# Low halves of woven weights by an adding DMA, with a changed planner, in a two-layer encoder trunk

## The chip, the cores and the metric

The kernel runs on one core of a Trainium2 chip. The metric is the device time of one execution in microseconds. The kernel before takes 1692.75 us (median of three runs, 1692.19 to 1692.83). Besides these times there is one profiled execution, from which all rows below are taken.

Engine names as in the profile: PE is TensorE (matrix products; PEld its weight loads), DVE is VectorE, ACT is ScalarE, POOL is GpSimd, SP is SyncE, which issues the DMAs.

## The reference

Two requests of 512 tokens by 1024 features go through two layers with the same weights. Cut to what matters:

```python
# layer 0: RWKV-7 time mixing, in both directions
r, k, v = lerp(0) @ w_r, lerp(1) @ w_k, lerp(2) @ w_v
z = xn @ w_z
for d in range(2):                 # forward and backward, each its own decay and rate
    ys.append(_wkv7_scan(r, decay, k_d, v, -kk, kk * a, reverse=(d == 1)))
out = (group_norm(ys[0] + ys[1]) + bonus) * silu(z)
x = x + rms_norm(out @ w_o)
# layer 1: 2-D neighbourhood attention over an 8 x 64 grid
q, k, v, z = split(xn @ w_in + b_in, 4)
o = attention in a window of 8 x 16 tokens with a relative bias
x = x + rms_norm((o * silu(z)) @ w_ao + b_o)
```

All values are 32-bit floats. Every dense product here has 1024 x 1024 weights per output block of 1024 columns.

## The kernel before

A dense product is made of three products in a reduced 32-bit format: each operand x is split in a high half, x rounded to that format, and a low half, x minus the high half. High by high, high by low and low by high are summed in PSUM. A column of a dense product is 128 output features of 512 tokens. It takes 8 steps over the features, with 3 products of 128x128 by 128x512 each. Its weights come as two loads of 128x512 (256 KB) into tiles `raw` (three buffers). Each load is split into a pair `whi`, `wlo` (four buffers of each, `NW`), which serves four steps.

There are 144 columns for the two requests' projections, and the last output projections beside them. They run in three stages:

- A prelude (to about 172 us): norms, token shifts, the small low-rank products, and two sets of columns for the first request.
- The woven stage (172 to 1172 us). The scan of layer 0 runs in 8 groups (two requests, four blocks of heads) of 8 steps each. `prep` makes the scan's operands for a head pair, `inverse` inverts triangular blocks by elimination (lines 941 and 942, 30 dependent pairs of VectorE instructions per group), and `step` runs one scan step (products L1106, L1112, L1133, L1153 and L1157, with ScalarE's copies Z and X between them and VectorE's state S). `finish` normalises a group. Beside all this `flow` makes 76 columns of dense products: r and v of the first request, k, r, v and z of the second, the first request's output projection of layer 0, and the first `NPA` of eight sets of four columns of its layer-1 input projection. `NPA` is 5.
- The rest (1172 to 1694 us): the remaining columns, and attention, whose steps are given out between products at fixed rates (`POST0` 0.7 steps per step of an input column, `POST` 1.0 per step of an output column; what is left comes behind them).

The order of PE, DVE and ACT in the woven stage is written out by a planner. Each piece of work is a Python generator, a `Thread` with a rank. A `yield` names the engine of what comes next, and may give a gate (a condition that must hold) and a time at which operands are ready. `weave` keeps a `Clock` with modelled costs and ends of every instruction. It gives the next turn to a thread whose work can start about now, engines other than PE first, then by rank. Products of `flow` have the rank 9 and so fill what the scan leaves free. `Clock.LAT` is what the model adds between an engine's end and a reader on another engine; `one` holds the costs per instruction (`n` is the number of elements per partition). The queues of SP and POOL are not written out: the building library sets their order.

`splits` in `flow` is the part that the change is about. A half may be split once its load is issued and the pair four halves back has been used (`did["k"] // 4 + NW`). ScalarE copies `raw` into the high half (L703). VectorE subtracts it from `raw` into the low half (L705). Only then may `products` set the steps that read it (L751 to L753). `splits` has rank 3 when no more than one half is in stock, else 9. POOL has only small memsets in this stage: the padding column of `prep`'s exponentials (L841) and parts of `MT` (L959).

In the rest the same split is made by `halves` (L355, L356), and the products by `gemm` (L406 to L408); neither is changed.

Of the kernel before, what the change touches and what calls it, by code (L numbers as in the profile page):

```python
# [11 lines left out]
F32 = mybir.dt.float32  # L12
F32R = mybir.dt.float32r
AF = mybir.ActivationFunctionType
ALU = mybir.AluOpType
# [4 lines left out]
P = 128  # L20
T = 512
D = 1024
# [28 lines left out]
class Clock:  # L51
# [1 line left out]


    ENG = {"PE": "P", "Activation": "A", "DVE": "D", "Pool": "G", "SP": "S"}
    LAT = dict(P=200.0, A=45.0, D=45.0, G=90.0, S=0.0)
    BANKS = ("pf", "zy", "us", "pm", "pg", "pt", "po")

    def __init__(self, nc):
# [52 lines left out]
    def one(self, e, i):  # L112
        ap = lambda xs: [x for x in xs if hasattr(x, "bass_ap")]
        outs, ins = ap(i.outs), ap(i.ins)
        if not outs:
            return 0.0
        name = lambda x: x.bass_ap.tensor.name
        t = issued = self.t[e]
        for table, xs in ((self.made, ins), (self.used, outs)):
            for x in xs:  # L120
                for f, at in table.get(name(x), {}).items():
                    if f != e or e == "S":
                        t = max(t, at)
        free = lambda x: int(np.prod([n for _, n in x.ap[1:]])) if len(x.ap) > 1 else 1
        n = max([free(outs[0])] + [free(x) for x in ins[:1]])
        if e == "P":
            t, done = self.matmul(i, ins, free(outs[0]), t)
        elif e == "S":

            self.t[e] = issued = max(issued, self.t["P"]) + 380.0  # L130
            size = outs[0].ap[0][1] * free(outs[0]) * 4
            c = size * 0.0027 + 150.0
            self.dq = max(issued + 800.0, self.dq) + c
            done = max(self.dq, t + 800.0 + c) + 670.0
        else:
            if e == "A":
                c = 175.0 + 0.86 * n
            elif e == "G":
                c = 150.0 + n
            else:  # L140
                kind = type(i).__name__
                sb = [x for x in ins if free(x) > 8 and not name(x).startswith(self.BANKS)]
                c = 80.0 + 1.06 * n
                if "Reciprocal" in kind:
                    c = 80.0 + 6.2 * n
                elif getattr(i, "is_tensor_tensor_scan", False):
                    c = 80.0 + 2.1 * n
                elif "Transpose" in kind:
                    c = 80.0 + 1.8 * n
                elif len(sb) == 1 and len(ins) <= 2 and "TensorTensor" not in kind and "Reduce" not in kind and free(outs[0]) == n:  # L150
                    c = 110.0 + 0.53 * n if not getattr(i, "is_scalar_tensor_tensor", False) else 130.0 + 1.06 * n
            self.t[e] = t + c
            done = t + c + self.LAT[e]
        for x in ins:
            u = self.used.setdefault(name(x), {})
            u[e] = max(u.get(e, 0.0), done)
            self.slot[name(x)] = True
        for x in outs:
            for table in (self.used, self.made):
                u = table.setdefault(name(x), {})  # L160
                u[e] = max(u.get(e, 0.0), done)
        return 0.0 if e == "S" and "dram" in str(type(outs[0].bass_ap.tensor)).lower() else done
# [51 lines left out]

class Trunk:
    NACT, NW, NRAW, NXR, NTMP, WP = 18, 4, 3, 3, 5, 512
    POST0, POST, POST2, POST3, NPA = 0.7, 1.0, 0.15, 0.66, 5
    HP, HS = (1000, 0), 1000
    OUT1 = ("pg", "pg", "pg", "pg")
    HPA = 1000  # L220
# [460 lines left out]
    def flow(self):  # L681


        nc, did, ck = self.nc, self.did, self.clock
        cols = [(g, j, src, done) for g, (_, _, c) in enumerate(self.groups) for j, (src, done) in enumerate(c)]
        name = lambda *xs: [x.tensor.name for x in xs]
        raw, w, x, todo = {}, {}, {}, {}
# [11 lines left out]
        def splits():  # L699
            for h in range(2 * len(cols)):  # L700
                yield "A", lambda: h < did["load"] and h < did["k"] // 4 + self.NW, lambda c: c.at(name(raw[h]))
                hi, lo = (self.t(tag, (P, self.WP), self.NW, F32R) for tag in ("whi", "wlo"))
                nc.scalar.copy(hi, raw[h])  # L703
                yield "D"
                nc.vector.tensor_tensor(lo, raw.pop(h), hi.bitcast(F32), op=ALU.subtract)  # L705
                w[h] = hi, lo
                did["split"] += 1

# [50 lines left out]
        def posts(a):  # L759
# [4 lines left out]

        few = lambda: did["split"] - did["k"] // 4 <= self.STOCK
        return [
            Thread(lambda: 0, loads()), Thread(lambda: 3 if few() else 9, splits()), Thread(lambda: 0, fetched()), Thread(lambda: 2.5, operands()),
            Thread(lambda: 9, products()), Thread(lambda: 2, posts(0)), Thread(lambda: 2, posts(1))]


    def prep(self, s, p):
# [139 lines left out]
        ks = kps[0]  # L911
        yield "D"
        vt.tensor_tensor(ks, kps[0], kps[1], op=ALU.add)
        vt.scalar_tensor_tensor(ks, ks, self.vec("rk", p), r, op0=ALU.mult, op1=ALU.mult)
        self.save("ks", s, p, ks)

# [5 lines left out]
    def inverse(self, s, pb):  # L922

        nc = self.nc
        vt, gps, act = nc.vector, nc.gpsimd, nc.scalar
        f = lambda tag, shape: self.t(tag, shape, 1, F32, self.front)
        wc, Gd, Go = self.formed[s, pb]
        NU = 32
        free, room = self.bank()
        need = lambda *xs: lambda c, n=[x.tensor.name for x in xs]: c.at(n)  # L930
        gd, go = (x.rearrange("p h i g t -> p (h i g) t") for x in (Gd, Go))
        yield "D", None, need(Gd)
        N = f("N", (P, 32, 32))
        vt.transpose(N, gd.rearrange("p u t -> p t u"))
        tmp = f("etmp", (P, 256))
        self.did["gd"] += 1
        for q in range(1, 31):
            n = 31 - q
            tv = tmp[:, :n * q].rearrange("p (i j) -> p i j", i=n)
            yield "D"  # L940
            vt.tensor_tensor(tv, N[:, q + 1:, q:q + 1].broadcast_to([P, n, q]), N[:, q:q + 1, :q].broadcast_to([P, n, q]), op=ALU.mult)  # L941
            vt.tensor_tensor(N[:, q + 1:, :q], tv, N[:, q + 1:, :q], op=ALU.add)  # L942
        yield "D"
        vt.tensor_tensor(N, N, self.lower, op=ALU.mult)
        vt.memset(N.rearrange("p i j -> p (i j)")[:, 0:1024:33], 1.0)

        yield "D"
        NA = f("NA", (P, NU, 32))
        vt.transpose(NA.rearrange("p u j -> p j u"), N.rearrange("p i j -> p j i"))
        MT = self.MTb[self.nM % 2]  # L950
        self.nM += 1

        yield "D"
        vt.transpose(MT[:, :, 0, :].rearrange("p u i -> p i u"), N)
        yield "A"
        for q in (1, 3):
            r = slice(32 * q, 32 * q + 32)
            act.copy(MT[r, :, 1], MT[r, :, 0])
            gps.memset(MT[r, :, 0], 0.0)  # L959
        for step in range(2):  # L960
            for j0 in (0, 16):
                us = slice(j0, j0 + 16)
                yield "P", free, (lambda c: max(room(c), need(NA)(c))) if step == 0 else (lambda c: max(room(c), need(MT)(c)))
                ps = self.p("pm", (P, 16, 32))
                for j in range(16):
                    for h in range(2):
                        x, y = slice(64 * h, 64 * h + 32), slice(64 * h + 32, 64 * h + 64)
                        u = j0 + j
                        if step == 0:
                            nc.tensor.matmul(ps[y, j], go[x, u], NA[x, u], start=True, stop=True, tile_position=(64 * h, 64 * h + 32))  # L970
                        else:
                            nc.tensor.matmul(ps[x, j], NA[y, u], MT[y, u, 1], start=True, stop=True, tile_position=(64 * h + 32, 64 * h))
                yield "A", None, need(ps)
                for h in range(2):
                    if step == 0:
                        y = slice(64 * h + 32, 64 * h + 64)
                        act.copy(NA[y, us], ps[y])
                    else:
                        x = slice(64 * h, 64 * h + 32)
                        act.copy(MT[x, us, 1], ps[x])  # L980
        self.formed[s, pb] = wc, MT
# [98 lines left out]
    def step(self, q):  # L1080
# [16 lines left out]
        ab, e = st.ab, st.e  # L1097
# [60 lines left out]
        if not st.last:  # L1158
# [3 lines left out]
            if st.i == 0:  # L1162
                vt.tensor_tensor(st.S, so, wc, op=ALU.mult)
            else:
                vt.tensor_tensor(st.S, so, before.S, op=ALU.add)
                vt.tensor_tensor(st.S, st.S, wc, op=ALU.mult)

        yi = st.y[:, min(st.i, 7 - st.i)]
# [11 lines left out]
    def finish(self, s, pb, y):  # L1180
# [14 lines left out]
        bc = lambda t: t.unsqueeze(2).broadcast_to([P, 16, HD])  # L1195
        yield "D", None, need(y)
        vt.tensor_reduce(st[:, 0], yv, axis=AX.X, op=ALU.add)
        vt.tensor_scalar(st[:, 1], st[:, 0], -1.0 / HD, None, op0=ALU.mult)
        yield "D"
        vt.tensor_tensor(yv, yv, bc(st[:, 1]), op=ALU.add)  # L1200
# [654 lines left out]
```

## Time and profile before

| what | value |
|---|---|
| median of the runs shown | 1692.75 us |
| profiled execution | 1695.69 us, span 1693.9 us |
| mean granted TensorE clock | 0.958 |
| PE, DVE, ACT, POOL busy in the span | 91%, 73%, 58%, 1% |
| PE busy in the woven stage, 172 to 1172 us | 879.44 us of 1000 |
| moved by DMA | 336.23 MB, 198 GB/s on the mean |

In a row of a group stand its line, engine, operation and tiles, its shape and count, then busy us and mean ns of one, and the idle time of its engine just before, with what ended it. In a row of waits stand who waited, for whom, us in total, times, and the longest. A row of a stretch gives busy us of each engine with the number of instructions, then the granted clock, the share of the DMA engines and GB/s. A row of DMA issues ends with the median us from issue to landing. Busy times of one group are those of a profiled execution whose PE ends are modelled.

### The profile page before, as it was taken

How to read it: one execution, taken by the hardware profiler on the slowest of the kernel's cores; microseconds unless marked ns; L12 is line 12 of the kernel's file. 1: busy time of each engine (PE TensorE's matmuls, PEld its weight loads, DVE VectorE, ACT ScalarE, POOL GpSimd, SP SyncE). 2: the span in 40 equal slices, each digit the busy share in tenths (PEclk: the TensorE clock that was granted, in tenths of full speed). 3: DMA queues.
4: the chain of work that ended last, by engine and by line, in shares of the span. 5: the costliest groups of instructions: out<-in, count | busy, mean ns of one | idle time of the engine just before them, and what ended most of it. 6: DMA issues, size and time to landing. Idle time of an engine off the chain costs nothing.

```text
span 1693.9 us, 45876 instructions
## 1 busy us (share of the span) xinstructions
PE 1542.3 (91%) x18624; PEld 1171.7 (69%) x18624; DVE 1243.6 (73%) x2725; ACT 987.9 (58%) x1979; POOL 24.1 (1%) x94
## 2 busy tenths in 40 slices
PE   7989788889998988889978689999999999999998
PEld 6767556666676766666656477777777887777776
DVE  8985679688786886897878988656566686555564
ACT  5443655767665666667576545544567765555562
POOL 0000000000000000000000000000000000000000
PEclk9989989899999999999989799999999999999999
DMA  5435687786686777885667754557555346545553
GB/s 207 162 124 187 201 286 222 209 257 224 196 258 197 233 230 220 273 262 188 210 226 233 225 181 141 158 169 261 177 184 181 113 138 240 188 155 174 168 175 106
DMA packets 240819, 336.23 MB, mean 198 GB/s; under 512 B 53696, under 2 KB 119360, under 8 KB 240608
## 3 DMA queue, kind: packets, MB, share of 16 engines
q1 hardware_dynamic: 240608, 333.31, 61.2%
q8 instruction: 146, 2.39, 0.6%
q14 instruction: 65, 0.53, 0.1%
HBM read 227.71 MB, written 105.51 MB: 197 GB/s over the span
## 4 chain that ended last, share of the span: by engine, by line
PE 59%; DVE 16%; DMA 9%; ACT 9%; issue 5%; SPq 1%; DVEq 0%; ACTq 0%
PE pg L406 6%; PE pg L407 6%; PE pg L408 6%; PE pm L751 5%; PE pm L752 4%; PE pm L753 4%; PE sc L1375 2%; PE pf L1035 2%; PE po L1408 2%; DVE etmp L941 2%; DVE N L942 2%; PE pt L1393 1%; PE zy L1106 1%; DVE wlo L705 1%; PE us L1133 1%
## 5 line engine op out<-in xcount | busy, mean ns | idle before, releaser
L751 PE MATMUL pm<-act,whi 128*128 128x512 f32 x608 | 272.5, 448 | 19.4 <-ACT whi L703 8.9
L753 PE MATMUL pm<-act,wlo 128*128 128x512 f32 x608 | 249.2, 410 | 13.3 <-DVE wlo L705 11.9
L752 PE MATMUL pm<-act,whi 128*128 128x512 f32 x608 | 248.6, 409 | 11.2 <-DVE act L731 8.3
L406 PE MATMUL pg<-act,whi 128*128 128x512 f32 x480 | 199.8, 417 | 0.0
L407 PE MATMUL pg<-act,whi 128*128 128x512 f32 x480 | 190.2, 396 | 0.0
L408 PE MATMUL pg<-act,wlo 128*128 128x512 f32 x480 | 189.8, 396 | 0.0
L355 ACT CAST whi<-raw 128x512 fp32r<-128x512 f32 x156 | 96.4, 619 | 134.8 <-PE pg L407 87.9
L751 PEld LDWEIGHTS pm<-act,whi 128*128 128x128 f32 x608 | 119.2, 196 | 60.5 <-issue 13.3
L753 PEld LDWEIGHTS pm<-act,wlo 128*128 128x128 f32 x608 | 119.3, 196 | 50.0 <-DVE wlo L705 19.4
L356 DVE TENSOR_TENSOR wlo<-raw,whi 128x512 fp32r<-128x512 f32 x156 | 106.7, 686 | 59.8 <-ACT whi L355 49.8
L752 PEld LDWEIGHTS pm<-act,whi 128*128 128x128 f32 x608 | 119.7, 197 | 34.8 <-DVE act L731 11.4
L705 DVE TENSOR_TENSOR wlo<-raw,whi 128x512 fp32r<-128x512 f32 x152 | 103.3, 684 | 46.8 <-ACT whi L703 43.7
L703 ACT CAST whi<-raw 128x512 fp32r<-128x512 f32 x152 | 93.1, 618 | 31.4 <-PE pm L752 13.1
L408 PEld LDWEIGHTS pg<-act,wlo 128*128 128x128 f32 x480 | 90.7, 189 | 19.9 <-issue 0.7
L406 PEld LDWEIGHTS pg<-act,whi 128*128 128x128 f32 x480 | 90.9, 189 | 19.4 <-issue 4.8
L407 PEld LDWEIGHTS pg<-act,whi 128*128 128x128 f32 x480 | 91.0, 190 | 17.2 <-issue 3.0
L942 DVE TENSOR_TENSOR N<-etmp,N 128x30 f32<-128x30 f32 (+14 forms) x240 | 79.7, 332 | 8.2
L941 DVE TENSOR_TENSOR etmp<-N 128x30 f32<-128x30 f32 (+14 forms) x240 | 78.4, 327 | 4.5
L1386 DVE CUSTOM_DVE_ANT_0 sb<-sc,bias 128x256 f32<-128x256 f32 x128 | 50.5, 420 | 39.8 <-PE pt L1393 29.2
L1389 ACT ACTIVATE sb<-sb,mx 128x256 f32<-128x256 f32 x128 | 64.2, 503 | 16.4 <-DVE mx L1388 16.0
L1035 PE MATMUL pf<-cab 64*64 64x128 f32 (+1 forms) x2048 | 69.9, 274 | 3.7 <-issue 3.1
L1145 ACT COPY X<-us 64x256 f32<-64x256 f32 x128 | 46.8, 366 | 33.7 <-PE zy L1013 31.2
(381 smaller groups left out, 3298.3 us busy)
## 6 DMA issues: line engine op xcount, KB each, us to landing
dab<-ab SPq DMA_DIRECT2D x32, 1024.0 KB, 7.3
cab<-dab SPq DMA_DIRECT2D x64, 512.0 KB, 4.3
raw<-in_w_in_dram SPq DMA_DIRECT2D x128, 256.0 KB, 3.4
bias<-in_rpb_dram SPq DMA_DIRECT2D x32, 384.0 KB, 4.1
raw<-in_w_z_dram SPq DMA_DIRECT2D x32, 256.0 KB, 5.3
dz<-tmp SPq DMA_DIRECT2D x32, 256.0 KB, 3.3
raw<-in_w_k_dram SPq DMA_DIRECT2D x32, 256.0 KB, 2.6
dk<-tmp SPq DMA_DIRECT2D x32, 256.0 KB, 3.1
```

Source lines behind the costliest of these rows:

```text
L355: self.nc.scalar.copy(hi, src)
L356: (eng or self.nc.vector).tensor_tensor(lo, src, hi.bitcast(F32), op=ALU.subtract)
L406: nc.tensor.matmul(ps, hi, x[k][0], start=(k == 0), stop=False)
L407: nc.tensor.matmul(ps, hi, x[k][1], start=False, stop=False)
L408: nc.tensor.matmul(ps, lo, x[k][0], start=False, stop=(k == KT - 1))
L705: nc.vector.tensor_tensor(lo, raw.pop(h), hi.bitcast(F32), op=ALU.subtract)
L751: nc.tensor.matmul(ps, hi[:, at], xh, start=(k == 0), stop=False)
L752: nc.tensor.matmul(ps, hi[:, at], xl, start=False, stop=False)
L753: nc.tensor.matmul(ps, lo[:, at], xh, start=False, stop=(k == KT - 1))
L941: vt.tensor_tensor(tv, N[:, q + 1:, q:q + 1].broadcast_to([P, n, q]), N[:, q:q + 1, :q].broadcast_to([P, n, q]), op=ALU.mult)
L942: vt.tensor_tensor(N[:, q + 1:, :q], tv, N[:, q + 1:, :q], op=ALU.add)
L1035: end = nc.tensor.matmul(st.f[half(a), h, 0, d, g] if st.last else st.f[half(a), h, :, d, g], ab[half(h), d, g, 2 * e[d] + 1 - a], rt if s ...
```

## The change

The low half in `splits` is made in two steps. ScalarE writes the negated rounding of `raw` into the low tile. Then POOL issues a DMA that reads the same 256 KB of weights from DRAM a second time and adds them onto that tile in SBUF. `raw` is free after ScalarE's second reading. The planner treats a DMA on POOL's queue like one on SP's.

The other edits: `NPA` goes from 5 to 7, so that 84 columns are woven and eight fewer are left to the rest. The planner's latencies and costs of ScalarE and VectorE are changed; and on those two engines a reader on the same engine now waits for the modelled latency as well. Five pairs of dependent VectorE instructions get a `yield` between them, so that the planner may put other work there. The rank of `operands` goes from 2.5 to 0.6.

```diff
-    LAT = dict(P=200.0, A=45.0, D=45.0, G=90.0, S=0.0)
+    LAT = dict(P=210.0, A=125.0, D=116.0, G=120.0, S=0.0)
...
-                    if f != e or e == "S":
+                    if f != e or e == "S" or e in "AD" and table is self.made:
...
-        elif e == "S":
+        elif e == "S" or e == "G" and "DMA" in type(i).__name__:
...
-                c = 175.0 + 0.86 * n
+                c = 85.0 + 0.85 * n
...
-                c = 80.0 + 1.06 * n
+                c = 82.0 + 1.02 * n
...
-    POST0, POST, POST2, POST3, NPA = 0.7, 1.0, 0.15, 0.66, 5
+    POST0, POST, POST2, POST3, NPA = 0.7, 1.0, 0.15, 0.66, 7
...
                 nc.scalar.copy(hi, raw[h])
-                yield "D"
-                nc.vector.tensor_tensor(lo, raw.pop(h), hi.bitcast(F32), op=ALU.subtract)
+                yield "A"
+                nc.scalar.mul(lo, raw.pop(h), -1.0)
+                yield "S"
+                c, j = divmod(h, 2)
+                nc.gpsimd.dma_start(lo, cols[c][2][:, j * self.WP:(j + 1) * self.WP], accum_op=ALU.add)
                 w[h] = hi, lo
...
-Thread(lambda: 2.5, operands()),
+Thread(lambda: 0.6, operands()),
...
             vt.tensor_tensor(tv, N[:, q + 1:, q:q + 1].broadcast_to([P, n, q]), N[:, q:q + 1, :q].broadcast_to([P, n, q]), op=ALU.mult)
+            yield "D"
             vt.tensor_tensor(N[:, q + 1:, :q], tv, N[:, q + 1:, :q], op=ALU.add)
```

The other four `yield "D"` stand in `prep` (before L914), in `inverse` (before L945), in `step` (before L1166) and in `finish` (before L1198).

More of the change, by code (lines that the diff above doesn't have):

```diff
@@ L766, in flow @@
         return [
-            Thread(lambda: 0, loads()), Thread(lambda: 3 if few() else 9, splits()), Thread(lambda: 0, fetched()), Thread(lambda: 2.5, operands()),
+            Thread(lambda: 0, loads()), Thread(lambda: 3 if few() else 9, splits()), Thread(lambda: 0, fetched()), Thread(lambda: 0.6, operands()),
             Thread(lambda: 9, products()), Thread(lambda: 2, posts(0)), Thread(lambda: 2, posts(1))]
@@ L941, in inverse @@
             vt.tensor_tensor(tv, N[:, q + 1:, q:q + 1].broadcast_to([P, n, q]), N[:, q:q + 1, :q].broadcast_to([P, n, q]), op=ALU.mult)
+            yield "D"
             vt.tensor_tensor(N[:, q + 1:, :q], tv, N[:, q + 1:, :q], op=ALU.add)
@@ L944, in inverse @@
         vt.tensor_tensor(N, N, self.lower, op=ALU.mult)
+        yield "D"
         vt.memset(N.rearrange("p i j -> p (i j)")[:, 0:1024:33], 1.0)
@@ L1165, in step @@
                 vt.tensor_tensor(st.S, so, before.S, op=ALU.add)
+                yield "D"
                 vt.tensor_tensor(st.S, st.S, wc, op=ALU.mult)
@@ L1197, in finish @@
         vt.tensor_reduce(st[:, 0], yv, axis=AX.X, op=ALU.add)
+        yield "D"
         vt.tensor_scalar(st[:, 1], st[:, 0], -1.0 / HD, None, op0=ALU.mult)
```

## The prediction

> **What bounds the kernel now.** I read the page's busy shares first, then three stretches of the span: the prelude, the hand-planned stage in which scan and products are woven (172 to 1172 us, from the first woven product to the last), and the rest.
>
> ```profile
> span 1693.9 us, 45876 instructions
> PE 1542.3 (91%) x18624; PEld 1171.7 (69%) x18624; DVE 1243.6 (73%) x2725; ACT 987.9 (58%) x1979; POOL 24.1 (1%) x94
> 0.00:172.00 172.00, 154.37 (x625) 116.12 (x626) 140.32 (x263) 81.62 (x139) 1.86 (x44) 0.96 0.49 171
> 172.00:1172.00 1000.00, 879.44 (x15156) 655.57 (x15157) 784.92 (x1497) 613.21 (x1193) 22.27 (x50) 0.94 0.69 219
> 1172.00:1694.00 522.00, 508.47 (x2846) 399.96 (x2844) 318.41 (x968) 293.04 (x650) 0.00 (x0) 0.99 0.52 168
> 200.00:300.00 100.00, 82.46 (x814) 62.15 (x814) 78.72 (x145) 59.93 (x119) 2.45 (x7) 0.92 0.80 253
> ```
>
> The columns of a stretch are busy us of PE, weight loads, DVE, ACT and POOL, then the granted clock, the share of the DMA engines and GB/s. TensorE is the bound. It is busy 97% of the rest (508.5 of 522), but leaves 120.6 us of the woven stage empty at a clock of 0.94; there DVE is the next fullest engine (78%) and the DMA engines the one after (69%; 80% in the fullest of seventeen stretches of 100 us). What can be won lies in the woven stage. Who ends TensorE's waits there:
>
> ```profile
> PE pm L753 <- DVE wlo L705: 11.9, 14, 4.2
> PE pm L751 <- ACT whi L703: 8.9, 5, 5.4
> PE pm L752 <- DVE act L731: 8.3, 5, 4.0
> PE pm L1227 <- DVE bv L1221: 5.5, 2, 3.2
> PE pm L1227 <- DVE y L1212: 4.6, 3, 2.8
> PE zy L1106 <- DVE y L1173: 4.6, 5, 1.3
> PE us L1133 <- ACT Z L1118: 4.0, 7, 0.9
> PE pm L751 <- ACT act L728: 4.0, 1, 4.0
> PE zy L1112 <- DVE N L942: 4.0, 1, 4.0
> PE us L1153 <- ACT X L1145: 3.5, 6, 1.2
> ```
>
> Each row gives us in total, times and the longest. The largest is the very instruction that the change takes from DVE, the low halves of the weights; the second is the high halves. Many short waits make up the rest: it is an order of work that comes late by a little in many places.
>
> **The change part by part.** The prices:
>
> ```profile
> L751 PE MATMUL pm<-act,whi 128*128 128x512 f32 x608 | 272.5, 448 | 19.4 <-ACT whi L703 8.9
> L753 PE MATMUL pm<-act,wlo 128*128 128x512 f32 x608 | 249.2, 410 | 13.3 <-DVE wlo L705 11.9
> L752 PE MATMUL pm<-act,whi 128*128 128x512 f32 x608 | 248.6, 409 | 11.2 <-DVE act L731 8.3
> L406 PE MATMUL pg<-act,whi 128*128 128x512 f32 x480 | 199.8, 417 | 0.0
> L407 PE MATMUL pg<-act,whi 128*128 128x512 f32 x480 | 190.2, 396 | 0.0
> L408 PE MATMUL pg<-act,wlo 128*128 128x512 f32 x480 | 189.8, 396 | 0.0
> L705 DVE TENSOR_TENSOR wlo<-raw,whi 128x512 fp32r<-128x512 f32 x152 | 103.3, 684 | 46.8 <-ACT whi L703 43.7
> L703 ACT CAST whi<-raw 128x512 fp32r<-128x512 f32 x152 | 93.1, 618 | 31.4 <-PE pm L752 13.1
> ```
>
> (a) Eight columns of the input projection move from the rest into the woven stage (NPA 5 to 7): 64 steps of three products. Woven they cost 64 x (0.448 + 0.409 + 0.410) = 81 us, in the rest they cost 64 x (0.417 + 0.396 + 0.396) = 77 us. Net +4.
>
> (b) The subtraction leaves DVE: 103 us go, and with eight more columns' readings (8 at about 0.68 us, taken like the subtraction's 0.684) DVE has about 688 us to do in the stage instead of 785. In the order of the built program the halves now stand far earlier: between the place of the DMA and the first product that reads its tile lies TensorE work of 16.4 us in the median, and under 6 us for 15 of 168 halves (products counted from the order, each group priced at its busy time over its count). Before, between the subtraction and that product, it is 7.0 us in the median and under 6 us for 69 of 152. So I let both split waits go, 11.9 + 8.9: -21.
>
> (c) DVE's other large waits above, 8.3 + 5.5 + 4.6 + 4.6 + 4.0 = 27.0 us, should shrink as its idle share grows from 22% to about 34%: I take a third, -9 (bounds 0 and -27).
>
> (d) ScalarE gains 168 negated copies and 16 more high halves, 184 x 0.618 = 114 us, and some 12 us for the readings of the eight columns: from 613 to 739 us. Its quoted waits other than the split's, 4.0 + 4.0 + 3.5 = 11.5 us, grow by a third: +4 (0 to +12). In-order behind the new copies stand the scan's own copies Z and X (L1118, L1145), each on the chain of a scan step.
>
> (e) The planner's numbers: it had 175 + 0.86n ns for a ScalarE instruction, 615 ns for 512 elements, and 45 ns from an engine's end to its reader. The timeline shows that ScalarE starts the next copy while the last one is still out:
>
> ```profile
> 481.88 0.62 ACT L726 CAST act<-xr 128x512 fp32r<-128x512 f32 x1
> 482.40 0.62 ACT L703 CAST whi<-raw 128x512 fp32r<-128x512 f32 x1
> ```
>
> 0.52 us apart, where the new formula says 85 + 0.85 x 512 = 520 ns. A plan that is nearer to the trace sets fewer products where something is not ready. Its order bears that out in part: 1909 products instead of 1776 stand before the last product of the scan. No row prices a plan; what can go is the stage's remaining idle time, 120.6 - 21 - 27 = 73 us, and nothing is the other bound. A plan that trusts in early transfers can also misplace work, so I take a little over a quarter: -20. The extra places at which the plan may put other work between two dependent DVE instructions go with it.
>
> (f) The DMA. 168 transfers of 256 KB are added on POOL's queue, which adds weights from DRAM onto the tile in SBUF. What is on the engines today:
>
> ```profile
> q1 hardware_dynamic: 240608, 333.31, 61.2%
> raw<-in_w_in_dram SPq DMA_DIRECT2D x128, 256.0 KB, 3.4
> raw<-in_w_v_dram SPq DMA_DIRECT2D x32, 256.0 KB, 5.6
> cab<-dab SPq DMA_DIRECT2D x64, 512.0 KB, 4.3
> ```
>
> 333.31 MB took 61.2% of 1693.9 us, so 256 KB (0.262 MB) take 0.82 us of all sixteen engines. The trace has no adding transfer. It reads two streams and writes one; the nearest row is the plain load. Lower bound once its time (168 x 0.82 = 137 us), upper bound four times (548 us); I take one and a half times, 1.22 us, 206 us. The stage's own demand is 690 us and, with 16 loads and 8 stores more, 710 us; with the new transfers 916 us of a stage of about 1040, a share of 0.88. That is above anything in the stretches, so I charge +12 for scan operands (cab) that land later (0 to the rival below). Nothing is taken below nothing: no transfer is removed. Landing: 3.4 to 5.6 us for a plain load; with POOL's issue I take 6 us. Summed over the 15 halves with less cover, 22 us are missing, and one stall gives the next halves time: +10 (0, if landing is 4 us, to the rival below).
>
> On POOL's queue the DMAs stand among the padding memsets, which wait for DVE today:
>
> ```profile
> POOL e L841 <- DVE ab L864: 615.1, 27, 51.1
> ```
>
> These long waits are POOL with nothing else to do. In the new order every memset waits for a DVE instruction that stands, in the order of the plan, ahead of the next DMA's own operand, so I cost that queue at nothing; SP's queue keeps its raw loads and carries 24 issues more in the stage, which the rest had.
>
> A rule of the Trainium skill speaks against a DMA on this queue: SBUF — State Buffer, in its section "SBUF: two separate sides", has POOL's descriptor writing locked out while DVE runs a two-port copy or tensor_scalar, and sends such transfers to another queue. What DVE has of these in the woven stage:
>
> ```profile
> L442 DVE TENSOR_SCALAR tmp<-cc,rs 128x128 f32<-128x128 f32 x8 | 1.7, 282 | 0.1
> L1198 DVE TENSOR_SCALAR st<-st 128x16 f32<-128x16 f32 x8 | 1.4, 174 | 0.3
> ```
>
> By that rule the sum would grow by at most these 3.1 us; no run here shows a DMA on this queue yet.
>
> (g) The rest. Its attention is fed step by step beside the products: 16 steps for each of 8 heads' pairs, 128 in all. Before, twelve input columns at 0.7 per step of products and eight output columns at 1.0 gave 96 x 0.7 + 64 = 131, all covered. Now it is 32 x 0.7 + 64 = 86, so 42 steps, 2.6 pairs, come after the covering products; in the built order only 45 products (18 us) are strewn among the last three. A pair's softmax on DVE:
>
> ```profile
> L1386 DVE CUSTOM_DVE_ANT_0 sb<-sc,bias 128x256 f32<-128x256 f32 x124 | 49.0, 420 | 37.7 <-PE pt L1393 29.2 <-PE sc L1375 6.9 <-DMA raw<-in_w_in_dram 0.4
> L1391 DVE TENSOR_SCALAR sb<-sb,mx 128x256 f32<-128x256 f32 x128 | 44.1, 351 | 2.5
> ```
>
> Eight times (0.420 + 0.351) is 6.2 us, with its small reciprocal and the reading of the result some 10 us: 26 us for 2.6 pairs, of which the 18 us of products cover most. Bounds 0 and +26; I take +10.
>
> (h) Clock. With the stage's idle falling by some 30 us net, the granted clock should rise from 0.94 by about a point and a half: 960 us of products x 0.015 = -15 (0 to -48, which is 0.99 as in the rest).
>
> Sum: 4 - 21 - 9 + 4 - 20 + 12 + 10 + 10 - 15 = -25. The profiled execution took 1695.7 us, its span and 1.8 us around it, 2.9 above the median 1692.75 of the runs shown: 1692.75 - 25 = 1668 us. The woven stage would then last 1668 + 2.9 - 1.8 - 172 - (522 - 77 + 10) = 1042 us.
>
> **Rivals.** 1. The DMA engines become the bound, and the kernel is slower. Place: the woven stage. Price: (710 + 168 x t) us at a share of at most 0.95. At t of two and a half times 0.82 the stage needs (710 + 344) / 0.95 = 1109 us, which gives 1735 us; at four times it would be far worse. It decides above a stage of 1067 us, t = 1.81 us or 2.2 times a plain load. For it: 0.80 in one stretch already with TensorE at 82%; two read streams. Against: no stretch shows where the engines stop, and one and a half times stays below it.
>
> 2. The low halves land late and hold TensorE, whose order is fixed. At a landing of 9 us 33 halves are short by 90 us in all, at 12 us 51 halves by 215 us. With the same share of it real as in (f), 10 of 22, that is +41 and +98 instead of +10: 1699 and 1756 us. It decides from about 8.5 us. Against it stand all landings above; for it, that POOL's issue has no row.
>
> 3. The wait only moves: DVE's relief is no use because ScalarE, at 71%, ends the same waits, and the plan is no better. Then (b), (c), (e) and (h) shrink to some -25 and the costs stay: about 1692 to 1710 us, say 1700.
>
> 4. More is won: long gaps vanish and the clock with them. TensorE: Matmul & The Clock Gate, Part 1, has the clock halved after an idle window of about 3.4 us, and the two split rows above have longest waits of 4.2 and 5.4 us, which agrees with a clock of 0.94 in this stage and 0.99 in the rest. From rows alone: (h) at -38 rather than -15 and (e) at -50 make 1668 - 23 - 30 = 1615 us.
>
> **How the numbers follow.** Forecast 0.44, the larger win 0.10, engines full 0.22, late landing 0.14, moved wait 0.10. The first two are faster, and so are a few of the others' mild ends: 0.55 faster. Within 0.2% (3.4 us, about what a measurement of this kernel can tell from no change) 0.04. Slower 0.41. The likeliest case alone lies between 1640 and 1688 us; the range must reach both signs, from the larger win to the late landing at 12 us: 1612 to 1756.
>
> **What would show it.** Right: no DVE-released wait at the low product and hardly a DMA-released one; TensorE busy for over 92% of a woven stage of about 1040 us; DVE near 690 us there; a DMA share near 0.88; landings near 6 us; the rest near 455 us. Wrong: low products that wait for the adding DMA by tens of us, a share of 0.95 with cab landing late, ScalarE at the head of TensorE's waits, or an attention stretch without products in the rest.

## The result and the profile after

The changed kernel takes 1801.86 us (median of 4 runs), the kernel before 1692.47 us beside it: a ratio of 1.066 (95% interval 1.0615 to 1.0706). It is slower by 6.6%, where I had forecast 1668 us, and lies above my range.

The page of the changed kernel: the span, the busy times, the DMA queues, and the three groups of woven products with the copies that feed them.

```profile
span 1795.3 us, 46213 instructions
PE 1578.0 (88%) x18624; PEld 1200.4 (67%) x18624; DVE 1133.6 (63%) x2557; ACT 1068.8 (60%) x2145; POOL 169.3 (9%) x262
q1 hardware_dynamic: 240608, 333.31, 57.4%
q0 software_dynamic: 24192, 44.05, 14.7%
L754 PE MATMUL pm<-act,whi 128*128 128x512 f32 x672 | 307.1, 457 | 16.3 <-ACT act L731 5.5
L756 PE MATMUL pm<-act,wlo 128*128 128x512 f32 x672 | 281.7, 419 | 33.0 <-DMA wlo<-in_w_r_dram 17.8
L755 PE MATMUL pm<-act,whi 128*128 128x512 f32 x672 | 280.1, 417 | 13.4 <-DVE act L734 11.4
L703 ACT CAST whi<-raw 128x512 fp32r<-128x512 f32 x168 | 103.5, 616 | 86.6 <-PE pm L755 71.6
```

The queue q0 is the new one: 44.05 MB in 24192 packets, 14.7% of sixteen engines' span. That is 0.147 x 1795.3 / 168 = 1.57 us of all sixteen per transfer, against 0.82 us for a plain load of the same size. The woven stage and the rest as stretches (PE, weight loads, DVE, ACT, POOL, clock, DMA share, GB/s), with the two fullest hundreds of microseconds:

```profile
172.00:1301.00 1129.00, 958.09 (x15386) 718.87 (x15387) 696.03 (x1367) 712.43 (x1391) 166.41 (x217) 0.91 0.86 241
1301.00:1795.00 494.00, 466.00 (x2615) 365.74 (x2613) 298.61 (x930) 273.88 (x614) 0.00 (x0) 0.97 0.50 161
600.00:700.00 100.00, 90.25 (x1621) 68.39 (x1618) 69.64 (x142) 69.54 (x139) 14.31 (x19) 0.93 0.96 265
700.00:800.00 100.00, 83.24 (x1440) 62.50 (x1439) 75.83 (x153) 65.44 (x135) 10.70 (x15) 0.93 0.94 269
```

The whole loss is in the woven stage: it grew from 1000 to 1129 us, and the rest shrank from 522 to 494. DVE came down to 696 us and ScalarE up to 712, where the prediction had 688 and 739. But TensorE's idle time in the stage rose from 120.6 to 170.9 us and its clock fell from 0.94 to 0.91. The DMA engines are busy for 0.86 of the stage, and nearly always between 600 and 800 us. The largest waits of VectorE and TensorE for transfers in the stage:

```profile
DVE ab L867 <- DMA dab<-ab: 24.0, 5, 7.5
PE pm L756 <- DMA wlo<-in_w_r_dram: 17.8, 6, 6.2
DVE rb L805 <- DMA k<-dk: 13.9, 2, 12.1
DVE bv L1229 <- DMA bv<-dv: 12.5, 5, 4.3
PE zy L1019 <- DMA cab<-dab: 8.9, 6, 3.4
```

In the kernel before the two largest are:

```profile
DVE bv L1221 <- DMA bv<-dv: 13.4, 4, 5.4
DVE ab L864 <- DMA dab<-ab: 3.9, 3, 2.5
```

So not only the low tiles are late: the store of the scan's operands (dab) and the scan's own operands (cab) are too. The reload of v (bv) was waited for as long before, and the 13.9 us for k stand beside 11.5 in g0 below, which has none of the added transfers. In all, DVE waits 56 us for transfers in the stage instead of 26, and TensorE 50 us instead of 2.

### The profile page after: what moved, and what is told of

Same layout as the page of the kernel before. It is cut to its first block, busy times and chain, and to the rows that moved or that the text cites. A ratio compares the mean times of both kernels' runs of the same rounds, so it can differ in the third digit from the quotient of the medians.

```text
span 1795.3 us, 46213 instructions
## 1 busy us (share of the span) xinstructions
PE 1578.0 (88%) x18624; PEld 1200.4 (67%) x18624; DVE 1133.6 (63%) x2557; ACT 1068.8 (60%) x2145; POOL 169.3 (9%) x262
## 3 DMA queue, kind: packets, MB, share of 16 engines
q0 software_dynamic: 24192, 44.05, 14.7%
HBM read 271.75 MB, written 105.51 MB: 210 GB/s over the span
## 4 chain that ended last, share of the span: by engine, by line
PE 57%; DMA 12%; issue 12%; DVE 9%; ACT 8%; POOL 1%; SPq 0%; DVEq 0%; POOLq 0%; ACTq 0%
PE pg L406 5%; PE pg L407 5%; PE pg L408 5%; PE pm L754 5%; PE pm L756 4%; PE pm L755 4%; PE pf L1041 2%; PE sc L1383 2%; PE us L1159 2%; POOL wlo L708 1%; PE po L1416 1%; DMA cab<-dab 1%; PE zy L1112 1%; PE zy L406 1%; DMA dy<-bv 1%
## 5 line engine op out<-in xcount | busy, mean ns | idle before, releaser
L754 PE MATMUL pm<-act,whi 128*128 128x512 f32 x672 | 307.1, 457 | 16.3 <-ACT act L731 5.5
L756 PE MATMUL pm<-act,wlo 128*128 128x512 f32 x672 | 281.7, 419 | 33.0 <-DMA wlo<-in_w_r_dram 17.8
L755 PE MATMUL pm<-act,whi 128*128 128x512 f32 x672 | 280.1, 417 | 13.4 <-DVE act L734 11.4
L756 PEld LDWEIGHTS pm<-act,wlo 128*128 128x128 f32 x672 | 136.0, 202 | 71.1 <-DMA wlo<-in_w_r_dram 20.8
L754 PEld LDWEIGHTS pm<-act,whi 128*128 128x128 f32 x672 | 135.4, 202 | 64.3 <-issue 15.2
L406 PE MATMUL pg<-act,whi 128*128 128x512 f32 x416 | 172.5, 417 | 2.0 <-ACT act L355 2.0
L407 PE MATMUL pg<-act,whi 128*128 128x512 f32 x416 | 166.0, 399 | 0.7 <-DVE act L356 0.7
L408 PE MATMUL pg<-act,wlo 128*128 128x512 f32 x416 | 165.5, 398 | 0.0
L755 PEld LDWEIGHTS pm<-act,whi 128*128 128x128 f32 x672 | 136.1, 202 | 42.3 <-DVE act L734 15.0
L356 DVE TENSOR_TENSOR wlo<-raw,whi 128x512 fp32r<-128x512 f32 x140 | 96.1, 687 | 76.3 <-ACT whi L355 68.4
L705 ACT ACTIVATE wlo<-raw 128x512 fp32r<-128x512 f32 x168 | 105.6, 628 | 0.1
L406 PEld LDWEIGHTS pg<-act,whi 128*128 128x128 f32 x416 | 79.2, 191 | 19.1 <-issue 3.2
L407 PEld LDWEIGHTS pg<-act,whi 128*128 128x128 f32 x416 | 79.5, 191 | 16.6 <-issue 2.0
L945 DVE TENSOR_TENSOR etmp<-N 128x30 f32<-128x30 f32 (+14 forms) x240 | 78.5, 327 | 5.0
L1064 DVE TENSOR_TENSOR AK<-zy,cc 128x256 f32<-128x256 f32 x63 | 26.5, 420 | 79.2 <-PE zy L1019 74.5
L1397 ACT ACTIVATE sb<-sb,mx 128x256 f32<-128x256 f32 x128 | 64.1, 504 | 13.9 <-DVE mx L1396 13.8
```

The lines of the kernel that those rows point to most:

```text
L356: (eng or self.nc.vector).tensor_tensor(lo, src, hi.bitcast(F32), op=ALU.subtract)
L406: nc.tensor.matmul(ps, hi, x[k][0], start=(k == 0), stop=False)
L407: nc.tensor.matmul(ps, hi, x[k][1], start=False, stop=False)
L408: nc.tensor.matmul(ps, lo, x[k][0], start=False, stop=(k == KT - 1))
L705: nc.scalar.mul(lo, raw.pop(h), -1.0)
L754: nc.tensor.matmul(ps, hi[:, at], xh, start=(k == 0), stop=False)
```

## The experiments

Theory A was that the added transfers do the harm; rival B, that the new plan with its longer weave does. Times are medians; each is beside runs of the kernel before on the same chip (medians 1693.2 to 1694.6 us), and a ratio stands with its 95% interval. e2, e3, e7, g1, g3, g4 and g5 rest on two runs each.

**The subtraction back, all else new (e1).**

```diff
-                yield "A"
-                nc.scalar.mul(lo, raw.pop(h), -1.0)
-                yield "S"
-                c, j = divmod(h, 2)
-                nc.gpsimd.dma_start(lo, cols[c][2][:, j * self.WP:(j + 1) * self.WP], accum_op=ALU.add)
+                yield "D"
+                nc.vector.tensor_tensor(lo, raw.pop(h), hi.bitcast(F32), op=ALU.subtract)
```

> The changed kernel with one thing undone: the low half is VectorE's subtraction again, no DMA on POOL's queue; the new planner numbers and NPA 7 stay. Theory A (the adding DMA is the cost: it fills the DMA engines, lands late, and TensorE's waits and clock pay): the 50 us of DMA-released waits and most of the clock's loss in the woven stage go, woven stage near 1050 us instead of 1130, time 1700 to 1725 us. Theory B (the new plan and the longer weave are the cost, the DMA rides along): woven stage stays near 1110 us or more, time 1770 us or above.

Measured: 1711.8 us, ratio 1.0106 (1.0063 to 1.015). Undoing the split with its DMA, and nothing else, takes 90 of the 109 us back; 19 us stay. The stretches (same columns):

```profile
171.00:1208.00 1037.00, 931.57 (x15346) 701.58 (x15345) 788.01 (x1513) 626.36 (x1214) 22.31 (x50) 0.93 0.68 215
1208.00:1712.00 504.00, 476.41 (x2656) 372.83 (x2654) 303.49 (x951) 278.93 (x628) 0.00 (x0) 0.96 0.51 166
```

The woven stage is 1037 us instead of 1129, with a DMA share of 0.68. Theory A holds for the 90 us, B does not; the 19 us belong to the rest of the change, and f1 below finds them in the attention.

**The DMA alone on the kernel before (e2).** The kernel before with the edit of `splits` and the planner's line for DMAs on POOL's queue, nothing else.

> The kernel before with the adding DMA alone: old planner numbers, NPA 5, no new places for other work; the planner treats the DMA like one on SP's queue, as in the changed kernel. Theory A: slower than before by 60 us or more (1750 to 1800 us), DMA share of the woven stage near 0.85, waits of TensorE for the low tile of tens of us. Theory B: within 20 us of before, since DVE's relief pays for the traffic.

Measured: 1821.3 us, ratio 1.0759 (1.0693 to 1.0825), a loss of 127 us. Alone, the edit costs more than with the new plan.

```profile
172.00:1294.00 1122.00, 920.67 (x15167) 681.97 (x15167) 700.94 (x1355) 691.04 (x1346) 152.97 (x201) 0.89 0.83 231
L756 PE MATMUL pm<-act,wlo 128*128 128x512 f32 x608 | 256.8, 422 | 49.6 <-DMA wlo<-in_w_r_dram 16.8 <-DMA wlo<-in_w_in_dram 12.3 <-DMA wlo<-in_w_z_dram 7.8
```

Here TensorE stands idle for 49.6 us before low products, against 33.0 with the new plan. The like comparison is with e3 below, which has the new plan and the same number of columns: there the loss is 66 us and that idle time 30.9 us. So the new plan takes about half of the DMA's cost away, and what a transfer costs depends on the order around it.

**NPA 5 in the changed kernel (e3), and with the subtraction (e4).**

```diff
-    POST0, POST, POST2, POST3, NPA = 0.7, 1.0, 0.15, 0.66, 7
+    POST0, POST, POST2, POST3, NPA = 0.7, 1.0, 0.15, 0.66, 5
```

> The changed kernel with NPA 5 instead of 7, so that eight columns go back to the rest and cover attention there; the DMA stays. Both theories: the rest's gap (14 us of idle TensorE and a clock of 0.86 in one stretch of 50 us) goes, some 20 us less, 1775 to 1785 us. If the moved columns were the main cost it would be below 1730 us.

> Subtraction on VectorE and NPA 5: only the planner's numbers, ranks and new places for other work are left of the change. Theory A: 1685 to 1705 us, about the time before. Theory B: if the new plan as such is worse, 1730 us or more. If the new numbers help as I had forecast, 1660 to 1680 us.

Measured: e3 1760.2 us, ratio 1.0398 (1.0335 to 1.0461), 42 us less than the changed kernel and more than either theory had. e4 1696.2 us, ratio 1.0023 (1.0 to 1.0047). So the planner's numbers, ranks and new places by themselves bring nothing. The DMA costs 64 us between e4 and e3, where 152 transfers are issued, and 90 between e1 and the changed kernel, where 168 are. Why sixteen more transfers cost 26 us more was not tried.

**No DMA, but all that goes with it (g0).** In place of the DMA the planner books its modelled end, and issues nothing. This kernel and g1, g3, g4 and g5, which are built on it, leave the weights out of the low tiles: they hold the negated rounding alone, so their results are not those of the reference.

```diff
-                nc.gpsimd.dma_start(lo, cols[c][2][:, j * self.WP:(j + 1) * self.WP], accum_op=ALU.add)
+                self.clock.ghosted = self.clock.ghost(lo)
```

> The changed kernel without its DMAs: the planner still books one for each half, with the same modelled end, but none is issued, so the low tiles hold the negated rounding alone (the low-half products are computed on that, not on the weights' remainder). ScalarE's extra copies and DVE's relief stay, in nearly the same order. Theory A1 (the transfers do all the harm; relief and extra copies cancel): like e1, 1700 to 1725 us. Theory A2 (DVE's relief is worth something by itself and the transfers eat it too): 1660 to 1695 us. Theory C (ScalarE's extra copies, in order ahead of the scan's copies Z and X, are a cost of their own): 1735 us or more.

Measured: 1705.0 us, ratio 1.006 (1.0036 to 1.0084).

```profile
172.00:1204.00 1032.00, 916.35 (x15371) 695.48 (x15370) 694.41 (x1365) 710.64 (x1390) 22.32 (x50) 0.94 0.69 220
```

DVE's relief (694 us in the stage instead of 788 in e1) and ScalarE's extra copies (711 instead of 626) leave the stage at 1032 us against 1037: theory A1, they cancel. Of TensorE's waits in the stage DVE ends 46 us and ScalarE 57; in e1 it was 38 and 53. The relief buys no shorter wait.

**The traffic alone (g1, and paced, g3).** To g0, the same adding DMAs are put back, but onto scratch tiles in DRAM that nobody reads (in the changed kernel they end in SBUF); in g3 each also waits for ScalarE's copy of its half. The edit of g3 against the changed kernel, beside what g0 has:

```diff
+        self.side = [self.dram(f"side{n}") for n in range(8)]
...
-                nc.scalar.mul(lo, raw.pop(h), -1.0)
+                mul = nc.scalar.mul(lo, raw.pop(h), -1.0)
...
-                nc.gpsimd.dma_start(lo, cols[c][2][:, j * self.WP:(j + 1) * self.WP], accum_op=ALU.add)
+                one = nc.gpsimd.dma_start(self.side[h % 8][:, 0:512], cols[c][2][:, j * self.WP:j * self.WP + 512], accum_op=ALU.add)
+                self.after(one, [mul])
```

> As g0_no_dma (low tiles hold the negated rounding alone), with the same 168 adding DMAs of 256 KB on POOL's queue, but onto eight scratch tiles in DRAM that nobody reads: the traffic without anyone waiting for it (its destination is DRAM, so the writes go elsewhere than in the changed kernel). Theory contention: the woven stage suffers though no product waits, cab, V and the reloads land late: 50 us or more above g0, near the changed kernel. Theory lateness (TensorE's wait for the low tile is what costs): within 20 us of g0.

> As g1_traffic_only (low tiles hold the negated rounding alone; 168 adding DMAs of 256 KB onto scratch tiles in DRAM that nobody reads), but each DMA waits for ScalarE's negated copy of its half, as in the changed kernel, so that the traffic comes at the same pace and not in a heap at the start. Theory contention: 1780 to 1820 us, other transfers (cab, k, bv, the stores of ab) late, share near 0.85. Theory lateness, or the heap of g1 was the cause there: 1705 to 1725 us.

Measured: g1 1817.3 us, ratio 1.0731 (1.0688 to 1.0774). But without a wait POOL issued the transfers in a heap, and the DMA engines were full from the start of the span on, so g1 alone decides nothing. g3, paced: 1803.3 us, ratio 1.0649 (1.0628 to 1.0671), within 2 us of the changed kernel, though no product waits for any of these transfers.

```profile
172.00:1303.00 1131.00, 955.49 (x15370) 719.73 (x15369) 696.90 (x1368) 711.77 (x1390) 158.11 (x217) 0.91 0.87 240
q0 software_dynamic: 24192, 44.05, 15.8%
DVE ab L890 <- DMA dab<-ab: 35.7, 7, 8.1
DVE bv L1252 <- DMA bv<-dv: 29.4, 8, 8.1
DVE rb L828 <- DMA k<-dk: 21.3, 2, 16.7
PE zy L1042 <- DMA cab<-dab: 16.5, 9, 3.9
```

The stage, its clock and its share are those of the changed kernel. What waits is other work: the store of ab, the reloads of v and k, the scan's operands. The same four in g0:

```profile
DVE rb L824 <- DMA k<-dk: 11.5, 3, 6.1
DVE ab L886 <- DMA dab<-ab: 7.0, 3, 3.1
DVE bv L1248 <- DMA bv<-dv: 6.4, 4, 1.9
PE zy L1038 <- DMA cab<-dab: 1.4, 2, 0.7
```

From g0 to g3 the stage grows by 99 us. Of these, 60 are idle time of TensorE: its waits that a transfer ends grow from 1 to 23 us, those that DVE ends from 46 to 76, and those that ScalarE ends stay at 57. The other 39 are busy time, for the same products at a clock of 0.91 instead of 0.94. The theory of contention holds: the traffic costs by itself what the change costs. The late landing of the low tiles is not needed for it.

**The lateness known to the planner (e7).** The changed kernel, and in the planner:

```diff
+            if e == "G":
+                done = max(done, t + 9000.0)
```

> The changed kernel with one line more in the planner: a DMA on POOL's queue ends no earlier than 9 us after it starts, so no product is set before that. Theory lateness: TensorE's waits for the low tile (33 us) go, and with them clock; 1740 to 1765 us. Theory contention: other late transfers stay, 1780 us or more.

Measured: 1807.1 us, ratio 1.0671 (1.0625 to 1.0716). TensorE's largest group of waits for the low tile went from 17.8 to 8.8 us and nothing was gained; in the new order other waits took its place, for DVE and for other transfers:

```profile
PE pm L757 <- DVE act L736: 21.3, 8, 5.1
PE pm L758 <- DMA wlo<-in_w_r_dram: 8.8, 3, 7.1
PE zy L1021 <- DMA cab<-dab: 8.2, 9, 2.5
PE pm L1229 <- DMA ks<-dks: 6.1, 2, 3.4
```

**What of the traffic (g4, g5).** As g3, but plain copies (without the adding), and adding DMAs of 16 columns (8 KB) instead of 512.

> As g3_paced_add with plain copies of the same 256 KB on the same queue instead of adding ones (one read stream, not two). If it is the engines' time that counts and adding doubles it: about half of g3's loss over g0_no_dma, 1740 to 1765 us, and about 0.8 us of all sixteen engines per transfer against 1.57 in the changed kernel. If every DMA on this queue costs the same whatever it does: as g3.

> As g3_paced_add with 8 KB instead of 256 KB (16 of 512 columns): the same number of adding DMAs, descriptors and waits on POOL's queue, nearly no bytes. If bytes on the engines are the cost: within 10 us of g0_no_dma, 1700 to 1715 us. If POOL's issue (0.86 us each, with the padding memsets behind it) or the queue as such is the cost: 1750 us or more.

Measured: g4 1737.9 us, ratio 1.0263 (1.0221 to 1.0305); g5 1711.9 us, ratio 1.0109 (1.0088 to 1.0131). First the woven stage and the queue of g4:

```profile
172.00:1235.00 1063.00, 932.13 (x15364) 706.42 (x15363) 694.75 (x1364) 710.82 (x1388) 109.72 (x217) 0.92 0.79 254
q0 software_dynamic: 13440, 44.05, 8.0%
```

Then those of g5:

```profile
172.00:1209.00 1037.00, 921.88 (x15367) 697.71 (x15366) 693.40 (x1363) 710.58 (x1388) 158.08 (x217) 0.93 0.74 220
q0 software_dynamic: 24192, 1.39, 2.8%
```

A copy takes 0.080 x 1730.7 / 168 = 0.82 us of all sixteen engines, just as a plain load; g3's adding 0.158 x 1802.1 / 168 = 1.69 us. The number of DMAs, the descriptors and POOL's issue cost 7 us (g5 over g0). In all, the plain copies cost 33 us over g0 and the adding DMAs 98. Adding doubles the engines' time and triples the loss. Bytes to and from DRAM are not what differs: both kernels read 271.75 MB and write 149.55 MB of it, and g4 even moves more GB/s in the stage (254 against 240). The number of packets is not it either, for g5 has as many as g3. The Trainium skill's warning on POOL's descriptors beside DVE (SBUF — State Buffer, "SBUF: two separate sides") had no part in it that these runs could show: with the full number of small DMAs the loss is 7 us, and in the changed kernel POOL's DMA instructions take 0.86 us in the median and 1.22 us at most.

**Versions that might win (f1, f2).** e1 with attention given out faster in the rest, and the same with six column sets woven:

```diff
-    POST0, POST, POST2, POST3, NPA = 0.7, 1.0, 0.15, 0.66, 7
+    POST0, POST, POST2, POST3, NPA = 1.0, 1.5, 0.15, 0.66, 7
...
-    POST0, POST, POST2, POST3, NPA = 0.7, 1.0, 0.15, 0.66, 7
+    POST0, POST, POST2, POST3, NPA = 1.0, 1.0, 0.15, 0.66, 6
```

> Subtraction on VectorE, the new plan, NPA 7, and attention given out faster in the rest: POST0 1.0 and POST 1.5, so 32 x 1.0 + 64 x 1.5 = 128 steps stand beside products. If the uncovered steps are what e1 loses in the rest (504 us where 522 less eight columns at 5.5 us would be 478), the rest comes to 480 to 488 us and the time to 1685 to 1697 us; if not, 1710 us as e1.

> Subtraction on VectorE, the new plan, NPA 6, with POST0 1.0 and POST 1.0 (64 x 1.0 + 64 x 1.0 = 128 attention steps beside products): a version that may beat both kernels, since with NPA 5 the new plan ran out of products before the scan's end and with 7 it has more than the scan can hide. 1675 to 1690 us; 1695 us if the middle brings nothing.

Measured: f1 1689.3 us, ratio 0.9974 (0.9955 to 0.9993); f2 1697.2 us, ratio 1.0021 (1.0003 to 1.0039). The rest of f1:

```profile
1202.00:1687.00 485.00, 464.96 (x2655) 365.81 (x2653) 301.50 (x951) 278.36 (x628) 0.00 (x0) 0.98 0.53 172
```

It is 485 us instead of e1's 504: the uncovered attention steps were 19 us there. No adding DMA is left in f1 and f2. f1 is the only one below the kernel before, by 0.26%; the middle value 6 was a miss.

## Why the prediction was wrong

The step that failed is (f), the added transfers. The time of one was between my bounds: 1.57 us, 1.9 times a plain load, where I had taken one and a half times. The share came out near the forecast (0.88 said, 0.86 measured) by luck: with 1.57 us a transfer my stage of 1042 us would have had (710 + 168 x 1.57) / 1042 = 0.93, and only the longer stage brings it back to 0.86. What was wrong is what I let that share cost: +12 us for contention and +10 for late landing, where the traffic by itself costs 98 (g3 over g0). That is 76 of the 134 us by which the forecast fell short. The rest is mostly the gains (b), (c), (e) and (h), which did not come: without its 22 us for transfers my sum gives 1646 us, and g0 takes 1705. I had read the engines' share as a capacity, harmless below a limit of about 0.95, and rival 1 was built the same way: by its formula 1.57 us a transfer would still have been a win, since it set the loss from 1.81 us on. The mean share of the stage has no such limit: from 0.69 to 0.79 the stage lost 31 us, and from 0.79 to 0.87 another 68. The mean hides bursts. Cut into stretches of 5 us, the DMA engines were busy for 0.95 or more in 180 of 1000 us already before the change, in 205 of 1030 in g0, 350 of 1060 in g4, 600 of 1130 in g3 and 555 of 1125 in the changed kernel. The trace of the kernel before could have shown this.

The planner has written out an order in which loads and stores are due at fixed places. With fuller engines some of them land later than that, and TensorE's order cannot go round them. This happens all over the stage: cut at the same products into 24 pieces of 43 us of g0, g3 loses some 9 us or more in three of them and next to nothing in five, and the seven pieces in which its share is 0.95 or more lose 17 us together, of some 97. A late transfer may be felt in the next piece, so this does not say which burst did the harm.

TensorE's clock goes with its gaps. In g0, g4 and g3 it has 19, 23 and 32 gaps of over 2 us in the stage, and the trace has its clock at half speed for 120, 160 and 212 us (a mean of 0.94, 0.92 and 0.91). Whether the gaps alone lower it was not tried.

- (a) The net of the moved columns was near nothing, as said, but each side was twice too large. I had taken the rows' mean duration as a product's price. Products overlap. The timeline of the kernel before shows them 0.23 us apart while each lasts 0.39:

```profile
1210.18 0.39 PE L407 MATMUL pg<-act,whi 128*128 128x512 f32 x1
1210.41 0.40 PE L408 MATMUL pg<-act,wlo 128*128 128x512 f32 x1
1210.65 0.39 PE L406 MATMUL pg<-act,whi 128*128 128x512 f32 x1
1210.88 0.40 PE L407 MATMUL pg<-act,whi 128*128 128x512 f32 x1
```

  At this distance eight columns are 192 x 0.23 = 44 us, not 81 and 77; between neighbouring products of the woven stage the median distance is 0.23 us too. The Trainium skill has 216 ns for 512 columns from start to start at full clock (TensorE: Matmul & The Clock Gate, "Wait — 56ns, not 53.3ns?"); the trace agrees to within 7%.
- (b) The same error made the cover of the low halves look longer than it was. Counted in the built order at 0.23 us a woven product, the work between a DMA and its first reader is about 10 us in the median, not 16.4, and some 50 halves have under 6 us; even at the rows' prices it is some 30, where I had 15. Landings were 5.9 to 7.2 us in the median, as assumed. This fits TensorE's 33 us of idle time before the low product, where I had +10. But e7 and g3 show that this was not what set the time.
- (c), (d) DVE's relief and ScalarE's extra copies cancel (g0 1705.0 beside e1 1711.8, whose intervals overlap). That is the mechanism of rival 3, which I gave 0.10. That the change without its transfers stands at 1705 us, beside this rival's 1700, is luck: the 1700 holds +22 us for the transfers, and the 1705 some 19 us of uncovered attention, where I had +10.
- (e) The planner's numbers brought nothing by themselves (e4, ratio 1.0023), where I had -20. With the subtraction, TensorE's idle time before a low product was 13.3 us before and 1.0 us in e4; it came back as other waits, and in e4 the woven products ran out 38 us before the rest began.
- (g) The uncovered attention was real: 19 us (e1 to f1) where I had +10, inside my bounds.
- (h) The clock fell with the new gaps, to 0.91, instead of rising.
- The queue of POOL, which (f) cost at nothing, takes at most the 7 us of g5. The 3.1 us of DVE instructions listed for it leave out three small rows of the same kind, 1.2 us together; the sum does not change by that.

## What to carry to other kernels

A mean share of the DMA engines is not a limit below which transfers are free; look at the share in stretches of a few microseconds too. In a stage whose order is fixed in advance, price an added transfer by what the loads and stores already there can bear in lateness, and look first at which of them feed the long chain. An adding DMA of 256 KB cost the engines here about two plain ones, so it is a poor way to take 0.68 us from an engine that is not the bound. And a product's price is the distance from start to start, not the duration in its row.

## What the runs showed that I had not expected

An adding DMA of 8 KB over 128 partitions still takes 0.028 x 1708.9 / 168 = 0.28 us of all sixteen engines, a third of what a copy of 256 KB takes. And traffic that nobody waits for (g3) cost as much as the same transfers in the path of the products. Which of the late transfers costs most was not separated: the store of ab, the reloads and the scan's operands were never delayed one at a time.
